# Two decoder layers on one core: the sampled rows' convolution, gate and pool moved into the mixing stage, the queries of sampled attention in an earlier memory pool, outputs issued by ScalarE and GpSimd

## The chip, the core and the metric

The kernel runs on one core of a Trainium2 chip, in one launch. The metric is the device time in microseconds (us). Before the change the median of three runs is 1473.05 us (1468.88 to 1478.08). TensorE, written PE in the profile, does the matrix products; VectorE (DVE), ScalarE (ACT) and GpSimd (POOL) work elementwise; SyncE (SP) only issues transfers (DMA). Every engine takes its instructions in the order in which they stand in its own list.

## What is computed

One step of a decoder with two layers, for 512 prompt rows and for 32 sampled rows (8 sequences of 4 new rows each), with 1024 columns. Of the reference:

```python
z = rms_norm(x, p['g_mix_pre']) @ p['w_in']
a, ga, u, vb, q, k, v, xd = jnp.split(z, IN_SPLITS, axis=-1)          # 256 columns each
ya, conv_new = conformer_conv(a, ga, conv_prev, ...)   # h = a*sigmoid(ga); depthwise conv of width 31; LayerNorm; silu
yb, v_rows = chunk_sgu(gelu(u), gelu(vb), ...)         # u * (causal mix of LayerNorm(v) within a chunk + b)
yc = (rms_norm(attend(q, k, v, lam), ...) * (1.0 - lam_init)).reshape(B_, T, D_C)   # differential attention
yd, pool_new = pool_mix(xd, pool_prev, pos, ...)       # means over windows of 2, 4, 8, 16 rows, minus the row
x = x + rms_norm(jnp.concatenate([ya, yb, yc, yd], axis=-1) @ p['w_out'], p['g_mix_post'])
gate, up = jnp.split(rms_norm(x, p['g_ffn_pre']) @ p['w_gu'], 2, axis=-1)
x = x + rms_norm((silu(gate) * up) @ p['w_down'], p['g_ffn_post'])
```

The sampled rows have states from earlier steps: the last 30 rows of the convolution's input, the last 15 of the pool's, and 2048 cached keys and values per sequence, in pages that a table names. The states after the step, the new keys and values and the normalized rows of the gate are outputs too.

## The kernel before

**Stages.** A layer has two stages. The mixing stage (`mixing`, pools `mix{l}`) makes the input projection and the four mixers of the 512 prompt rows. The projection carries the sampled rows along; their columns land in `zs` (128 partitions x 32 rows). The FFN stage (pools `ffn{l}`, `smp{l}`) has a main generator `prompt` (output projection, gate and up, down) and a background generator `sample`, whose steps are mixed into the steps of `prompt`. All matrix products are in fp32 made of parts: a weight `raw` is rounded to `whi` (ACT, L194) and the rest goes to `wlo` (DVE, or POOL for one piece, L197); an activation is split in the same way (L351 and L352 in the mixers, L241 and L242 in `turn`). A product is three matmuls: hi by hi, hi by lo, lo by hi.

**The output projection.** `project_last` runs it in eight turns, a row tile t and a half of the columns each, in the order (0,0), (1,0), (0,1), (1,1), (2,0), (2,1), (3,0), (3,1). The eight contraction blocks are taken in the order yc, ya, yd, yb, as the mixers get done. Each half's weights come in four pieces: of the second half POOL subtracts two, DVE two. After both halves of a row tile `finish` normalizes it, adds the residual (L1319), writes the rows x to memory (L1320), squares and scales again (L1326, tile m) and `turn` transposes it for the FFN (L239). Gate and up then run in chunks of 256 columns, with matmuls of 128x256.

**The sampled rows before.** `sample` first opens the pool `smx{l}` and runs `sample_conv`, `sample_gate` and `sample_pool` beside the output projection. The convolution adds 31 taps for two blocks of 128 channels by one small DVE instruction each (L894 twice, L897 60 times, 128x32); then two transposes, LayerNorm (L345, L346, L177 on DVE, L178 on POOL, L906), two transposes (L909) and the activation on ACT (L911). When `prompt` has set "turned" (the row tiles are transposed), the pool `att{l}` opens and `sample_attention` runs: queries (`rep`, `qs`), the new keys and values, then 64 gathers of key and value pages (L1011, L1041, POOL), transposing copies (L1014, `kt`), scores (`sx<-kt,qs`).

**What sets the order.** The instructions are written in the order in which the generators yield, and a scheduler with a model of the engines' times orders them on every engine. Pools share the core's memory: a tile that lies where an older one lay waits for the older one's last reader. Transfers issued by SP stand in one list: weight loads (`raw`, `rws`, `rwo`), row loads and, before the change, nearly all outputs.

## Time and profile before

| | value |
|---|---|
| three runs | 1468.88 to 1478.08 us, median 1473.05 |
| profiled execution | 1468.52 us |
| its span, first to last instruction | 1466.7 us |
| PE busy in it | 1399.7 us, 95% |
| DVE, ACT, POOL busy | 819.1, 498.2, 252.2 us |

The profile shows one execution. Busy times of engines overlap; a line of waits gives the idle time of an engine and the instruction that ended it. PEclk is the clock granted to TensorE as a share of its full speed. Times in a timeline are from the start of the span.

### The profile page before, as it was taken

What the parts mean: (1) busy time and instruction counts of PE and PEld (TensorE: products, weight loads), DVE (VectorE), ACT (ScalarE), POOL (GpSimd) and SP (SyncE); (2) the same over time, 40 slices, a digit from 0 to 9 for tenths busy, and PEclk for the clock granted to TensorE, in tenths of its full rate; (3) what the DMA queues carried; (4) which work ended last, traced back from release to release, by engine and by line L of the source; (5) the groups of instructions that cost most, each with busy time, mean ns of one, the idle gap of its engine ahead of it and who ended that gap; (6) DMA issues with size and microseconds to landing.
All of it is one profiled execution on the core that took longest, in us unless ns stands there. A gap on an engine that the chain in (4) does not pass through costs nothing.

```text
span 1466.7 us, 22999 instructions
## 1 busy us (share of the span) xinstructions
PE 1399.7 (95%) x9274; PEld 1091.6 (74%) x9274; DVE 819.1 (56%) x1624; ACT 498.2 (34%) x978; POOL 252.2 (17%) x271
## 2 busy tenths in 40 slices
PE   6999898999999999999989997989999999999997
PEld 6987687766676777777789876877666677777775
DVE  4996677866424323433769856778664333333344
ACT  4346453322224221222433444543222332222231
POOL 1001155354200000000310011543542000000003
PEclk9999898999999999999999978999999999999999
DMA  6320335787759741323432203367877596213132
GB/s 206 101 88 30 125 129 181 266 292 274 263 179 298 230 137 58 106 67 130 151 123 73 73 29 123 126 218 250 307 277 272 182 300 212 99 58 115 58 133 90
DMA packets 155204, 235.60 MB, mean 161 GB/s; under 512 B 8880, under 2 KB 116410, under 8 KB 155098
## 3 DMA queue, kind: packets, MB, share of 16 engines
q1 hardware_dynamic: 136522, 166.76, 34.6%
q0 software_dynamic: 18432, 67.12, 12.6%
q8 instruction: 73, 1.20, 0.3%
q14 instruction: 33, 0.27, 0.1%
q10 hardware_dynamic: 144, 0.26, 0.0%
HBM read 222.07 MB, written 12.04 MB: 160 GB/s over the span
## 4 chain that ended last, share of the span: by engine, by line
PE 80%; DVE 9%; issue 4%; DMA 2%; ACT 2%; POOL 2%; another core or an unknown queue 1%; SPq 0%; POOLq 0%; DVEq 0%; ACTq 0%
PE acc L128 61%; PE sx L128 10%; PE ps L128 3%; PE s L128 3%; DVE sca L897 2%; DVE wlo L197 1%; PE oT L128 1%; DMA kr<-in_cache_k_dram,ik 1%; POOL rsw L178 1%; DVE m L1326 1%; ACT whi L194 1%; DVE x_t L1319 1%; PE ps L521 1%; PE ps L239 1%
## 5 line engine op out<-in xcount | busy, mean ns | idle before, releaser
L128 PE MATMUL acc<-xhi,whi 128*128 128x512 f32 (+2 forms) x1152 | 410.8, 358 | 3.1 <-issue 1.1
L128 PE MATMUL acc<-xhi,wlo 128*128 128x512 f32 (+2 forms) x1152 | 407.9, 354 | 1.0 <-issue 0.7
L128 PE MATMUL acc<-xlo,whi 128*128 128x512 f32 (+2 forms) x1152 | 407.4, 354 | 1.3 <-DVE xlo L242 1.1
L197 DVE TENSOR_TENSOR wlo<-raw,whi 128x1024 fp32r<-128x1024 f32 x172 | 216.5, 1265 | 187.4 <-ACT whi L194 185.9
L194 ACT CAST whi<-raw 128x1024 fp32r<-128x1024 f32 x178 | 184.8, 1048 | 381.6 <-PE acc L128 324.0
L128 PEld LDWEIGHTS acc<-xhi,whi 128*128 128x128 f32 x1152 | 221.1, 192 | 47.5 <-issue 13.3
L128 PEld LDWEIGHTS acc<-xhi,wlo 128*128 128x128 f32 x1152 | 221.1, 192 | 34.9 <-issue 8.7
L128 PEld LDWEIGHTS acc<-xlo,whi 128*128 128x128 f32 x1152 | 221.3, 192 | 32.8 <-issue 5.3
L128 PE MATMUL acc<-whi,h 128*128 128x512 f32 x704 | 225.4, 397 | 0.3 <-issue 0.3
L128 PEld LDWEIGHTS acc<-whi,h 128*128 128x128 f32 x704 | 132.0, 189 | 45.4 <-issue 11.8
L128 PE MATMUL acc<-wlo,h 128*128 128x512 f32 x352 | 139.2, 397 | 0.0
L1301 POOL TENSOR_TENSOR m<-m,g_g_ffn_post 128x512 f32<-128x512 f32 x14 | 20.0, 1435 | 509.1 <-ACT junk L1300 509.1
L1014 DVE STREAM_TRANSPOSE kt<-kr 128x1024 f32<-128x1024 f32 x64 | 78.3, 1232 | 40.5 <-remote 18.2
L427 DVE SCALAR_TENSOR_TENSOR cacc<-hext,pf,cacc 128x512 f32<-128x512 f32 x120 | 86.9, 746 | 0.8
L1011 POOL DMA_INDIRECT kr<-in_cache_k_dram,ik x64 | 68.6, 1072 | 101.8 <-DVE kt L1014 88.1
L128 PEld LDWEIGHTS acc<-wlo,h 128*128 128x128 f32 x352 | 66.5, 189 | 17.6 <-issue 4.1
L178 POOL TENSOR_TENSOR rsw<-rsw,mhalf 128x1 f32<-128x1 f32 (+2 forms) x62 | 37.3, 604 | 239.4 <-DVE rsw L177 223.4
L1041 POOL DMA_INDIRECT vr<-in_cache_v_dram,iv x64 | 62.1, 970 | 82.0 <-PE sx L128 66.5
L1370 DVE SCALAR_TENSOR_TENSOR th<-th,acc 128x512 f32<-128x512 f32 (+1 forms) x46 | 29.7, 645 | 80.7 <-PE acc L128 80.5
L128 PE MATMUL sx<-kt,qs 128*32 128x128 f32 x1024 | 49.9, 277 | 7.7 <-issue 6.1
L128 PEld LDWEIGHTS sx<-kt,qs 128*32 128x32 f32 x1024 | 30.7, 109 | 24.5 <-issue 18.8
L1179 DVE SCALAR_TENSOR_TENSOR sth<-sth,ps 128x64 f32<-128x64 f32 x22 | 4.8, 219 | 72.7 <-ACT sth L1178 72.7
(426 smaller groups left out, 1855.2 us busy)
## 6 DMA issues: line engine op xcount, KB each, us to landing
raw<-in_w_gu_dram SPq DMA_DIRECT2D x44, 1024.0 KB
raw<-in_w_down_dram SPq DMA_DIRECT2D x20, 1024.0 KB
rws<-in_w_gu_dram SPq DMA_DIRECT2D x40, 512.0 KB
raw<-in_w_in_dram SPq DMA_DIRECT2D x16, 1024.0 KB
raw<-in_w_out_dram SPq DMA_DIRECT2D x8, 1024.0 KB
rwo<-in_w_out_dram SPq DMA_DIRECT2D x16, 512.0 KB
rws<-in_w_down_dram SPq DMA_DIRECT2D x16, 512.0 KB
x<-x_t SPq DMA_DIRECT2D x12, 512.0 KB
```

The source lines that it names most:

```text
L128: T.matmul(out, lhsT, rhs, start=start, stop=stop)
L178: G.tensor_tensor(y, v, mhalf[:P, :n], op=ALU.pow)
L194: S.copy(hi, src)
L197: eng.tensor_tensor(lo, src, hi.bitcast(F32), op=ALU.subtract)
L239: T.transpose(ov[:, c, :], src[:P, 128 * (4 * b + c):128 * (4 * b + c) + 128], ident[:P, :P])
L427: V.scalar_tensor_tensor(a, hext[c][:, t:t + SEQ], pf[:, 8 + 2 * t + c:9 + 2 * t + c], a, op0=ALU.mult, op1=ALU.add)
L897: V.scalar_tensor_tensor(a[:, c], ext[:, c, :, t:t + 4], pf[:, 8 + 2 * t + c:9 + 2 * t + c], a[:, c], op0=ALU.mult, op1=ALU.add)
L1011: G.indirect_dma_start(out=kr, out_offset=None, in_=ck, in_offset=bass.IndirectOffsetOnAxis(ap=ik[:, s, bg:bg + 1], axis=0))
L1014: V.transpose(kt, kr)
L1041: G.indirect_dma_start(out=v.rearrange("p t e -> p (t e)"), out_offset=None, in_=cv, in_offset=bass.IndirectOffsetOnAxis(ap=iv[:, s, a:a + ...
L1301: (V if (t, half) == (3, 1) else G).tensor_tensor(m[t][:, hs], m[t][:, hs], gain[:, hs], op=ALU.mult)
L1370: V.scalar_tensor_tensor(th[:, :n], th[:, :n], 0.5, ou[:, :n], op0=ALU.mult, op1=ALU.mult)
```

## The change

1. `sample_conv`, `sample_gate` and `sample_pool` no longer have a pool of their own. `mixing` runs them as its last step, after its own flows, in tiles of the mixing pool that are free by then (`spare`: the places of the queries' and keys' splits; `spare_p`: the ring `p`).
2. The convolution's 62 tap instructions become, for each block and each half of the sequences, one product over overlapping windows (128 x 16 outputs x 31 taps, L912) and one sum over the taps (L913), and two additions of the bias (L915).
3. The queries, the new keys and their scores become `sample_queries`, which runs in a pool `sqa{l}` before "turned"; `sample_attention` follows in `att{l}`, inside of it. `oacc` and `onew` take the places of `rep` and `se`.
4. Outputs of keys, values, states and of the rows x (for the three uses of `finish` that have a gain g) are issued by ACT, the sampled rows' loads and one output by POOL, no longer by SP.

The diff, cut to its core:

```diff
-
-    def sample_pool(l, mp, cmn, pw):
+        active += [sample_conv(l, mp), sample_gate(l, mp), sample_pool(l, mp, pw)]
+        while active:
+            advance(1)
+
+
+    def spare(mp, tag, n):
+        return mp.tile([128, SEQ], F32, tag=tag, name="sm_" + tag)[:, :n]
+
+    def spare_p(mp):
+        return mp.tile([128, SEQ], F32, tag="p", bufs=PB, name="smp")
+
+    def sample_pool(l, mp, pw):
         pf, _ = PF[l]
-        st = cmn.tile([128, 512], F32, tag="pr", bufs=2, name="sst")[:120, :256]
-        SY.dma_start(st, A["state_pool"][l].rearrange("s t c -> (s t) c"))
-        ext = mp.tile([128, 2, NS, 19], F32, tag="spx", name="spx")
+        st = spare_p(mp)[:120, :256]
+        G.dma_start(st, A["state_pool"][l].rearrange("s t c -> (s t) c"))
+        ext = spare(mp, "k1l", 38 * NS).rearrange("p (c s t) -> p c s t", c=2, s=NS)
         for c in range(2):
...
-        SY.dma_start(O[9][l].rearrange("s t c -> (s t) c"), cn[:120, :256])
+        S.dma_start(O[9][l].rearrange("s t c -> (s t) c"), cn[:120, :256])
...
-        SY.dma_start(O[10][l].rearrange("s t c -> (s t) c"), v_s)
+        G.dma_start(O[10][l].rearrange("s t c -> (s t) c"), v_s)
...
-    def sample_conv(l, mp, cmn):
+    def sample_conv(l, mp):
         pf, _ = PF[l]
-        ext = mp.tile([128, 2, NS, 34], F32, tag="scx", bufs=1, name="scx")
+        ext = [spare(mp, tag, 34 * NS).rearrange("p (s t) -> p s t", s=NS) for tag in ("k0l", "k1h")]
         for hf in range(2):
-            st = cmn.tile([128, 512], F32, tag="pr", bufs=2, name="sst")[:120, :256]
-            SY.dma_start(st, A["state_conv"][l, 4 * hf:4 * hf + 4].rearrange("s t c -> (s t) c"))
+            st = spare_p(mp)[:120, :256]
...
-            SY.dma_start(O[8][l, 4 * hf:4 * hf + 4].rearrange("s t c -> (s t) c"), cn[:120, :256])
+            S.dma_start(O[8][l, 4 * hf:4 * hf + 4].rearrange("s t c -> (s t) c"), cn[:120, :256])
             yield
-        a = mp.tile([128, 2, NS, 4], F32, tag="sca", name="sca")
-        for c in range(2):
-            V.tensor_scalar(a[:, c], ext[:, c, :, 0:4], pf[:, 8 + c:9 + c], pf[:, c:c + 1], op0=ALU.mult, op1=ALU.add)
-        for t in range(1, CW):
-            for c in range(2):
-                V.scalar_tensor_tensor(a[:, c], ext[:, c, :, t:t + 4], pf[:, 8 + 2 * t + c:9 + 2 * t + c], a[:, c],
-                                       op0=ALU.mult, op1=ALU.add)
-            if t % 4 == 0:
+        h = spare(mp, "k0h", 8 * NS + 256)
+        a = h[:, :8 * NS].rearrange("p (c s t) -> p c s t", c=2, s=NS)
+        for c in range(2):
+
+            k = pf[:, 8 + c:9 + c]
+            taps_ = bass.AP(k.tensor, k.offset, [k.ap[0], (0, 4), (0, 4), (2, CW)])
+            for hf in range(2):
+                e = ext[c][:, 4 * hf:4 * hf + 4]
+                win = bass.AP(e.tensor, e.offset, [e.ap[0], (34, 4), (1, 4), (1, CW)])
+                pr = spare_p(mp)[:, :16 * CW].rearrange("p (s t j) -> p s t j", s=4, t=4)
+                V.tensor_tensor(pr, win, taps_, op=ALU.mult)
+                V.tensor_reduce(a[:, c, 4 * hf:4 * hf + 4], pr, axis=AX, op=ALU.add)
                 yield
+            V.tensor_scalar(a[:, c], a[:, c], pf[:, c:c + 1], None, op0=ALU.add)
         o = ps()
         for c in range(2):
             T.transpose(o[:NT, 128 * c:128 * c + 128], a[:, c].rearrange("p s t -> p (s t)"), ident)
         mean, r = ln_stats(mp, o[:NT, :256], NT, "m")
-        xn = mp.tile([NT, 256], F32, tag="scn", name="scn")
+        xn = h[:NT, 8 * NS:]
...
-        with tc.tile_pool(name=f"smx{l}", bufs=1, reuse_waits="tile") as mp:
+        with tc.tile_pool(name=f"sqa{l}", bufs=1, reuse_waits="tile") as qp:
             yield
-            flows = [sample_conv(l, mp, sp), sample_gate(l, mp, sp), sample_pool(l, mp, sp, PW[l])]
-            while flows:
-                for fl in list(flows):
-                    if next(fl, 0) == 0:
-                        flows.remove(fl)
-                yield
+            pre = yield from sample_queries(l, sp, qp)
             while "turned" not in share:
                 yield
-        with tc.tile_pool(name=f"att{l}", bufs=1, reuse_waits="tile") as ap:
-            yield from sample_attention(l, sp, ap, ys, share)
+            with tc.tile_pool(name=f"att{l}", bufs=1, reuse_waits="tile") as ap:
+                yield from sample_attention(l, sp, qp, ap, ys, share, *pre)
...
-    def sample_attention(l, cmn, sp, ys, share):
+    def sample_queries(l, cmn, sp):
+
...
+        return sc, gsub, rep, nn, onew
+
+    def sample_attention(l, cmn, qp, sp, ys, share, sc, gsub, rep, nn, onew):
+        pf, nlam = PF[l]
+        ik, iv = IX[l]
+        selsq = sc[:, S_SQ:S_SQ + 256].rearrange("p (s t) -> p s t", s=NS)
+        qs = sp.tile([128, 4, 4, 2, 32], F32, name="qs")
+        G.memset(qs, 0.0)
+        nm = sp.tile([128, NS], F32, name="nm")
...
         V.scalar_tensor_tensor(x_t, m[t], r, x_t, op0=ALU.mult, op1=ALU.add)
-        SY.dma_start(x_at(stage + 1)(128 * t, 128), x_t)
         if g is None:
+            SY.dma_start(x_at(stage + 1)(128 * t, 128), x_t)
             return
         junk = jp.tile([128, DM], BF16, tag="ft", bufs=2, name="junk")
         S.activation(junk, x_t, AF.Square, accum_out=ss[:, 3:4])
+        S.dma_start(x_at(stage + 1)(128 * t, 128), x_t)
```

**What moves on ACT**, layer 0, at the end of the mixing stage. Before: the casts of the last mixer outputs (`ya`, `yb`), then the four casts of the second half of the output projection's weights, then the evacuation of its first turns (L1296, L1300).

```order
L351 CAST ya<-cacc_466 128x512
L351 CAST yb<-uv 128x512 x2
L351 CAST ya<-cacc_827 128x512
L194 CAST whi<-raw 128x1024 x4
L1296 COPY m_2039<-acc 128x512
L1300 ACTIVATE junk,sumt<-m_2039 128x512
L1296 COPY m_2040<-acc 128x512
```

After, from the same cast of `ya`: `smp`, `sm_...` are tiles of the sampled mixers, L835 is the last step of the pool, L926 an activation at the end of the convolution; L1312 is L1296 of before.

```order
L351 CAST ya<-cacc_827 128x512
L810 COPY smp<-ps 120x256
L811 DMA out_dram<-smp 120x256
L899 COPY smp<-ps 120x256
L900 DMA out_dram<-smp 120x256
L899 COPY smp<-ps 120x256
L835 ACTIVATE zs<-ps,pf_84 128x32 x2
L900 DMA out_dram<-smp 120x256
L926 ACTIVATE zs<-ps,pf_84 128x32 x2
L194 CAST whi<-raw 128x1024 x4
L1312 COPY m_2187<-acc 128x512
```

Three copies, three issues of outputs and four activations of the sampled rows now stand ahead of the four casts. The second of these casts also waits for the last sum of the taps (L913), whose product lies in the same memory, and the third for the landing of a state that L900 writes.

**What moves on PE**, layer 0, from the end of turn (1,0) of the output projection (blocks `yb`) to turn (0,1) (blocks `yc`). Before:

```order
L128 MATMUL acc<-whi,yb 128x512 x2
L128 MATMUL acc<-wlo,yb 128x512
L128 MATMUL acc<-whi,yb 128x512
L128 MATMUL acc<-whi,yc 128x512
L128 MATMUL acc<-wlo,yc 128x512
L128 MATMUL acc<-whi,yc 128x512 x2
L128 MATMUL acc<-wlo,yc 128x512
L128 MATMUL acc<-whi,yc 128x512
```

After: L897 transposes the convolution's state, L128 with `sm_q1h,pw` is the pool, L918 and L924 are the transposes before and behind the convolution's LayerNorm.

```order
L128 MATMUL acc<-whi,yb 128x512
L128 MATMUL acc<-wlo,yb 128x512
L897 MATMUL ps<-cst,smp 120x128
L128 MATMUL ps<-sm_q1h,pw 128x32
L128 MATMUL acc<-whi,yb 128x512 x2
L128 MATMUL acc<-wlo,yb 128x512
L128 MATMUL acc<-whi,yb 128x512
L918 MATMUL ps<-cst,sm_k0h 32x128 x2
L924 MATMUL ps<-cst,sm_k0h 128x32 x2
L128 MATMUL acc<-whi,yc 128x512
L128 MATMUL acc<-wlo,yc 128x512
```

The convolution's transposes have come ahead of the first matmul of turn (0,1).

**What moves on POOL**, layer 0, at the first gathers of sampled attention. Before: `scf` are copies of the convolution's state, L178 the reciprocal roots (128x1 for row tiles, 32x1 for the convolution's LayerNorm).

```order
L886 COPY scf<-scx 128x120
L178 TENSOR_TENSOR rsw<-rsw,mhalf 128x1
L886 COPY scf<-scx 128x120
L178 TENSOR_TENSOR rsw<-rsw,mhalf 128x1
L178 TENSOR_TENSOR rsw<-rsw,mhalf 32x1
L957 MEMSET qs 128x1024
L1011 DMA kr<-in_cache_k_dram,ik_2602 128x1024 x3
L1041 DMA vr<-in_cache_v_dram,iv_2603 128x1024 x4
```

After: L1317 is the gain of the output projection (L1301 before), the last L178 are those of the last row tile.

```order
L178 TENSOR_TENSOR rsw<-rsw,mhalf 128x1
L197 TENSOR_TENSOR wlo<-raw,whi 128x1024 x2
L178 TENSOR_TENSOR rsw<-rsw,mhalf 128x1
L1317 TENSOR_TENSOR m_2190<-m_2190,g_g_mix_post 128x512
L178 TENSOR_TENSOR rsw<-rsw,mhalf 128x1 x2
L1006 MEMSET qs 128x1024
L1027 DMA kr<-in_cache_k_dram,ik_2658 128x1024 x3
L1057 DMA vr<-in_cache_v_dram,iv_2659 128x1024 x4
```

The gathers stood behind the root of the convolution's LayerNorm; they stand behind the two roots of the last row tile now, and the first of them waits for the scaling of that row tile (L1343, which is L1326 before). Of the 256-column matmuls of gate and up, 188 stand ahead of the first scores before, 89 after; 48 stand ahead of the last row tile's turn after.

## Rows read from the trace of the kernel before

**Rows 1.** Page, part 1: busy time, share of the span, instructions of the matrix engine.

```profile
PE 1399.7 (95%) x9274; PEld 1091.6 (74%) x9274; DVE 819.1 (56%) x1624; ACT 498.2 (34%) x978; POOL 252.2 (17%) x271
```

**Rows 2.** Busy time by stretch: stretch, its length, five engines, PEclk, DMA share, GB/s.

```profile
core 0: us, PE busy (x) PEld busy (x) DVE busy (x) ACT busy (x) POOL busy (x), PEclk, DMA share, GB/s
176.00:183.00 7.00, 3.78 (x11) 2.76 (x11) 4.68 (x9) 5.76 (x10) 0.00 (x0) 0.52 0.99 343
183.00:189.00 6.00, 6.00 (x28) 4.93 (x27) 3.72 (x2) 4.51 (x7) 5.57 (x2) 1.00 0.04 10
230.00:241.00 11.00, 8.12 (x38) 7.86 (x39) 10.89 (x34) 5.19 (x15) 4.31 (x7) 0.53 0.72 230
```

**Rows 3.** Waits of PE, 160 to 275 us (layer 0): total us, times, longest.

```profile
PE ps L128 <- DVE ybs L862: 4.1, 1, 4.1
PE acc L128 <- ACT ya L351: 3.2, 1, 3.2
PE sx L239 <- DVE m L1326: 1.1, 2, 0.9
```

**Rows 4.** Waits of PE, 890 to 1005 us (layer 1).

```profile
PE sx L239 <- DVE m L1326: 2.4, 2, 1.8
PE ps L887 <- POOL scf L886: 1.3, 1, 1.3
```

**Rows 5.** Timeline of PE: start us, us, instruction, [idle before <-releaser].

```profile
179.79 0.80 PE L128 MATMUL acc<-whi,ya 128*128 128x512 f32 x1 [3.22 <-ACT ya L351]
...
189.47 0.40 PE L128 MATMUL acc<-whi,yc 128*128 128x512 f32 x1
...
227.19 0.28 PE L128 MATMUL acc<-xhi,whi 128*128 128x256 f32 x1
227.31 0.28 PE L128 MATMUL acc<-xlo,whi 128*128 128x256 f32 x1
...
244.17 1.09 PE L239 MATMUL sx<-cst,m 128*128 128x128 f32 x8
```

**Rows 6.** Timeline of ACT.

```profile
180.69 0.61 ACT L351 CAST ya<-cacc 128x512 fp32r<-128x512 f32 x1
182.30 3.89 ACT L194 CAST whi<-raw 128x1024 fp32r<-128x1024 f32 x4 [1.00 <-DVE ya L352]
...
250.18 0.65 ACT L911 ACTIVATE zs<-ps,pf 128x32 f32<-128x32 f32 x2 [1.58 <-PE ps L909]
```

**Rows 7.** Timeline of POOL.

```profile
183.43 5.77 POOL L197 TENSOR_TENSOR wlo<-raw,whi 128x1024 fp32r<-128x1024 f32 x2 [7.87 <-ACT whi L194]
...
245.48 0.53 POOL L178 TENSOR_TENSOR rsw<-rsw,mhalf 32x1 f32<-32x1 f32 x1 [2.68 <-DVE rsw L177]
...
247.10 1.20 POOL L1011 DMA_INDIRECT kr<-in_cache_k_dram,ik  x1 [0.19 <-issue]
...
349.27 0.94 POOL L1011 DMA_INDIRECT kr<-in_cache_k_dram,ik  x1 [0.30 <-issue]
```

**Rows 8.** Timeline of DVE.

```profile
235.96 2.03 DVE L897 SCALAR_TENSOR_TENSOR sca<-scx,pf,sca 128x32 f32<-128x32 f32 x12
...
242.83 1.28 DVE L1326 SCALAR_TENSOR_TENSOR m<-x_t,rsw,g_g_ffn_pre 128x1024 f32<-128x1024 f32 x1
...
244.37 0.41 DVE L345 BATCH_NORM_STATS2 bn<-ps 32x6 f32<-32x256 f32 x1
...
246.69 0.52 DVE L906 TENSOR_SCALAR scn<-ps,ag,rsw 32x256 f32<-32x256 f32 x1
...
355.36 1.25 DVE L1014 STREAM_TRANSPOSE kt<-kr 128x1024 f32<-128x1024 f32 x1 [0.22 <-DMA kr<-in_cache_k_dram,ik]
```

**Rows 9.** One line each: count, ns min/median/max, first and last start, form.

```profile
L352 DVE TENSOR_TENSOR ya<-cacc,ya x4: 681/686/692, 179.8 to 915.5; 128x512 fp32r<-128x512 f32 x4
...
L993 DVE TENSOR_REDUCE nn<-pn x2: 387/388/390, 271.1 to 1000.4; 32x8 f32<-32x256 f32 x2
...
L1317 ACTq DMA_DIRECT2D out_dram<-x_t x1: 370/370/370, 1463.2 to 1463.2; - x1
```

87 lines of the change are left out of this document (42 added, 45 removed).

## The prediction, made before the change was run

> **What bounds the kernel now.** I read the page's busy times first. TensorE (PE) is busy 95% of the span [rows 1], so an edit on another engine is worth what it takes from PE's idle time, or adds to it. All the sampled rows' matmuls, transposes and queries stay, in another place; PE's own work is the same. So I went to the waits of PE in the stretch that the change touches, from the end of the mixing stage to the first sampled attention scores. Layer 0 waits 3.2 us for ya, the last mixer output; 4.1 us for ybs, a sampled intermediate; 1.1 us for m, the rows that enter the FFN [rows 3]. Layer 1 waits 2.4 us for m and 1.3 us for scf of the sampled convolution [rows 4]; its wait for ya, at the same place, is taken to be as long. Last the windows, for the granted clock [rows 2]. After the stop before 179.79 the mean over 176 to 183 is 0.52, which is the lower level, 1.2 GHz, nearly throughout; over 183 to 189 it is 1.00 again, 2.4 GHz. After the 4.1 us stop it is 0.53 over 230 to 241. In that stretch PE is busy 8.12 us; the same work at 1.00 is 8.12 x 0.53 = 4.3, so **one drop costs about 3.8 us**. A reader should see that a stop of 3 to 4 us here is paid nearly twice.
>
> The sum is made against the profiled execution's 1468.5 us, which is 0.3% under the median of the runs, 1473.05.
>
> **The change part by part.**
>
> *1. The gaps at the head of the FFN go.* With the sampled mixers gone from there, the waits for ybs and scf have no place: -4.1 in layer 0 with its clock drop of 3.8, -1.3 in layer 1. Together **-9.2 us**.
>
> *2. The taps.* 62 small instructions become four products and four sums over 496 columns and two additions. Twelve of the old ones took 2.03 us [rows 8], 0.17 each, so 62 take 10.5. The nearest product is 0.69 for 512 columns; the nearest sum is 0.39 for 256 columns [rows 9], which is 0.39 if the columns cost nothing and 0.75 if they cost everything. I take 0.6 for each of the eight, one behind the other, and 0.3 for the additions: 5.1. No row has an operand that reads overlapping windows; at double price the products add 2.8 us. So VectorE (DVE) is relieved of some 5 us per layer; alone that moves nothing but what waits for it, which part 3 counts. The Trainium skill ("VectorE: DVE Perf Modes", Rules for kernel authors) asks for the fewest instructions in a chain of DVE work, which speaks for this, and warns that tensor_reduce runs at the 1x rate and is the slowest DVE operation, which speaks against it. Its table's 2293 ns for a product of 2048 columns gives 0.56 for 496, an estimate; by that the taps would take some 0.3 us less than 5.1.
>
> *3. The second half of the output projection's weights.* This is where the change costs. Before, ScalarE (ACT) rounds them at 182.30, four casts in 3.89 us, right behind the cast of ya [rows 6]; GpSimd (POOL) subtracts the first two low halves from 183.43, 5.77 us for two [rows 7]; PE arrives at turn (0,1) at 189.47 [rows 5] and doesn't wait. In the order of after, three copies and four activations of the sampled mixers and three DMA issues stand on ACT between the cast of ya and these casts, the last of them L926, behind the convolution's LayerNorm. PE too has the convolution's two pairs of transposes, L918 and L924, ahead of the first matmul of turn (0,1). An engine goes through its rows in order, so the cast can't start before the whole chain of taps, LayerNorm and activation is through. (Also the second cast's memory is that of the last product.) Its times, layer 0:
> - ya: four small copies, some 0.2 each, go ahead of its cast on ACT, and of the thirteen sampled transposes and small matmuls ahead of it on PE the last waits for a copy on POOL that waits for these. I take 1.4 for both: PE starts ya at 181.2 instead of 179.79. The thirteen themselves fill the gap.
> - PE: the two turns took 9.7 (179.79 to 189.47). With 11 small sampled matmuls between, 0.12 each by the pitch of the FFN's [rows 5], 1.3, they end at 192.2.
> - DVE: the products can start when ya's split and about ten small instructions are done, some of which wait for sampled matmuls that stand behind half of the ya matmuls: I put that at 187.5 (185.5 if nothing is waited for, 189 if every one is). Taps done at 192.6, just behind PE.
> - From there: transposes 0.4, statistics 0.41, small steps 0.3, reciprocal root on POOL 0.53 [rows 7], normalization 0.52, transposes 0.4, five hand-overs of 0.1: 3.1. L926 takes 0.65, as L911 does [rows 6], to 196.4. First cast 0.97 (3.89 / 4): 197.4. First low half on POOL 2.9 (5.77 / 2): 200.3. Second: 203.2.
> - PE does one matmul of the new turn at 197.4 and then stands till 200.3, so from 192.2 to 200.3, less 0.7 for L918, L924 and that matmul: **7.4 idle**. Five more at 0.23 (the pitch is 9.7 us over some 42), and it needs the second low half at 201.7: **1.5**.
> - The clock drops after such a stop: **3.8**, as measured after the 3.2 and the 4.1.
> Per layer **+12.7**; both layers have the same order here: **+25.4 us**. Bounds: zero, if the chain ends 8.1 us sooner; 2.8 more for slow windowed products.
>
> *4. The sampled queries and the early pool.* Queries, new keys and the values' part now run before "turned", beside the FFN's first chunks. PE work is the same. The gathers of the attention wait (the pool shares memory) for the scaling of m3 (L1343 now, L1326 before). At the gather of the steady phase 6.1 us lie from issue (349.27) to the copy that waited for its landing at 355.36 [rows 7, 8]; the transposing copy takes 1.25. From the scaling of m3: memset and issue 1.3, landing 6.1, copy 1.25: 8.6. PE in that time: eight transposes 1.1, then 41 gate and up matmuls at 0.12 (after has the first scores behind 89 of these matmuls and the turn of m3 behind 48), 4.9: 6.0. So 2.6, and 0.7 for the next two pages, **3.3 idle per layer, +6.6**. Before, the first gather went out at 247.10 and nothing waited. Bound below: zero, if PE arrives late for another reason.
>
> *5. m.* Turn m3 stood 17.0 us behind the end of the output projection (227.19 to 244.17) [rows 5]. In after it stands behind 48 of the 256-column matmuls (5.8 us), and squares, gain, two roots, residual (1.28 each for full rows [rows 8]) don't fit in that. I take layer 1's present 2.4 [rows 4] for both: **+1.3** in layer 0, none in layer 1.
>
> *6. Outputs and loads on other queues.* 14 output issues per layer move to ACT at 0.37 each [rows 9], 5.2 us, and about seven sampled loads to POOL at around 1 (an indirect one takes 0.94 to 1.20 [rows 7]). POOL is 17% busy, ACT 34% [rows 1]. Three of them are ahead of the casts, 1.1 us, but the casts wait for the convolution anyway: nothing; if that cover is gone, 1.1 per layer. SyncE gets its weight loads sooner; no wait of PE in these stretches is for a weight load [rows 3, 4], so nothing. The Trainium skill ("DMA: Bandwidth & Descriptors", Issuing engines are not separate DMA queues) says of spreading only that it saves the issuing sequencer's time. No run here shows it yet.
>
> Sum: -9.2 + 25.4 + 6.6 + 1.3 = **+24.1, 1468.5 to 1492.6**, 1493. On the median of the runs it would be 1497.
>
> **The rivals.**
> - *A, faster, 1450.* The splits find the convolution done: L926 ends by 188.3 (192.2 less a cast and a low half, 3.9) instead of 196.4. Then only part 1 stays, -9.2, with the gap before ya filled by the sampled matmuls that now stand there (1.4 per layer) and the gap behind m in layer 1 gone, 2.4, and its second drop avoided, 3.8: 1468.5 - 18. For it: DVE is only 4.7 of 7 us busy before 183 [rows 2], and the short chain may be started before ya. Against it: the order puts the taps behind ya's low halves. 0.12.
> - *B, about the same, 1478.* The chain ends 5 us sooner, 3.9 of the 8.9 idle us remain, and the gathers are nearly in time. Layer 0: -7.9 + 3.9 + 3.8 + 1.3 = 1.1; layer 1: -1.3 + 3.9 + 3.8 = 6.4; with one page's copy awaited in each, 1.25, 1478.5. For it: the starting time of the taps is the weakest number above. 0.33.
> - *C, forecast, 1493* (1482 to 1501): 0.43.
> - *D, worse, 1506.* Windowed products at double price (+2.8 per layer) and the wait for the gathers pulls the clock down once more per layer (+3.8): 1492.6 + 13.2. 0.12.
> - That the output moves pay for themselves needs a PE wait for a load; there is none, so it has no chance of its own.
>
> **How the numbers follow.** The time is C's. From A's 0.12 the low end leaves all out but its edge, 1463; the high end, 1506, leaves out the upper half of D: 0.18 outside. Within 1% (about what a measurement can tell; 1458 to 1488 round the median) lie B and a quarter of C: 0.44. Slower: the rest of C and D, 0.44. Faster: A, 0.12.
>
> **What would show it.** In the profile of after: no PE wait for ybs or scf (part 1); four products of 0.6 to 0.7 and four sums of at most 0.75 (2); PE's largest wait in the stretch at turn (0,1), for the low halves on POOL or the casts, 7 to 9 us, with the granted clock near 0.5 behind it (3); PE waiting 2 to 4 us for kt before the first scores (4) and 2.4 for m (5). I'm wrong if the casts L194 start by 190, or if the stop there is there and the clock stays at 1.00.

## The result and the profile after

The changed kernel takes 1509.2 us (median of four runs, 1507.2 to 1510.5) against 1472.3 us of the kernel before on the same chip: a ratio of 1.0256 [1.0230, 1.0281], slower. On a second chip, where the kernel before takes 1442.5, it is 1476.9, 1.0249 [1.0227, 1.0271]. The forecast was 1493 with a range up to 1506: right in the direction, too small by a third (+24 us where +37 came), and the measured time lies outside the range. Chips differ by 2% in the kernel before, so every ratio below is to it on the same chip.

Two pairs of profiles are compared, one for each chip: the *first pair* (before 1466.7 us, after 1508.8) and the *second pair* (both kernels unedited, 1441.8 and 1470.6). The PE line of the first pair's changed kernel answers to [rows 1]:

```profile
PE 1424.0 (94%) x9274; PEld 1101.2 (73%) x9274; DVE 805.1 (53%) x1520; ACT 498.0 (33%) x978; POOL 270.3 (18%) x285
```

The 9274 matmuls are the same in number, and PE is busy 24.3 us longer with them. From the page and the line of spans and clocks:

| us | before | after | difference |
|---|---|---|---|
| first pair: span | 1466.7 | 1508.8 | +42.1 |
| of it PE busy / not busy | 1399.7 / 67.0 | 1424.0 / 84.8 | +24.3 / +17.8 |
| mean granted clock; (1 - clock) x span | 0.979; 30.8 | 0.968; 48.3 | +17.5 |
| second pair: span | 1441.8 | 1470.6 | +28.8 |
| of it PE busy / not busy | 1385.7 / 56.1 | 1400.1 / 70.5 | +14.4 / +14.4 |
| mean granted clock; (1 - clock) x span | 0.982; 26.0 | 0.980; 29.4 | +3.4 |

(1 - clock) x span is what the lower clock can have cost at most, if PE had work all that time; as the clock has three digits, it is good to about 1 us. Without it the pairs agree: +24.6 and +25.4 us. But a single execution says little about the clock's share. On the second chip the four executions of the changed kernel lose 29.4 to 39.8 us in this way (median 36.9), and the profiled one least; seven of the kernel before lose 18.7 to 31.7 (median 23.1). So of the 34.5 us between the medians there, up to 13.8 can be the clock's, not 3.4.

The waits of PE in the first pair's changed kernel (waited for; us, times, longest), first layer 0, 160 to 275 us as in [rows 3], then layer 1, 890 to 1040 us, since it is later there than in [rows 4]:

```profile
PE sx L128 <- issue: 4.2, 6, 1.2
PE acc L128 <- ACT whi L194: 3.6, 1, 3.6
PE sx L239 <- DVE m L1343: 2.8, 2, 1.7
...
PE ps L924 <- DVE sm_k0h L921: 2.2, 1, 2.2
...
PE acc L128 <- DVE wlo L197: 0.9, 1, 0.9
...
PE sx L128 <- issue: 5.0, 6, 1.8
PE acc L128 <- ACT whi L194: 4.6, 2, 3.6
PE ps L461 <- DVE xn L455: 3.5, 2, 2.8
PE ps L924 <- DVE sm_k0h L921: 2.2, 1, 2.2
PE ps L918 <- DVE sm_k0h L915: 2.2, 1, 2.2
```

The waits for ya, ybs and scf are gone. In their place PE waits for the casts `whi` of the second half of the output projection's weights, and for the end of the sampled convolution (L915, L921), which it has to pass first. How that comes about stands in the timeline of the same kernel, layer 0 (start, duration, engine, line, what; in brackets the idle time ahead of it and who ended it):

```profile
188.84 1.26 DVE L912 TENSOR_TENSOR smp<-sm_k0l,pf 128x496 f32<-128x496 f32 x2
190.02 1.25 DVE L912 TENSOR_TENSOR smp<-sm_k1h,pf 128x496 f32<-128x496 f32 x2
191.19 2.39 DVE L913 TENSOR_REDUCE sm_k0h<-smp 128x16 f32<-128x496 f32 x4
195.77 0.53 DVE L921 TENSOR_SCALAR sm_k0h<-ps,ag,rsw 32x256 f32<-32x256 f32 x1 [0.68 <-POOL rsw L178]
196.44 0.39 PE L924 MATMUL ps<-cst,sm_k0h 32*128 32x32 f32 x2 [2.19 <-DVE sm_k0h L921]
196.87 0.65 ACT L926 ACTIVATE zs<-ps,pf 128x32 f32<-128x32 f32 x2 [3.25 <-PE ps L924]
197.41 3.88 ACT L194 CAST whi<-raw 128x1024 fp32r<-128x1024 f32 x4
198.58 5.67 POOL L197 TENSOR_TENSOR wlo<-raw,whi 128x1024 fp32r<-128x1024 f32 x2 [2.85 <-ACT whi L194]
200.37 1.64 DVE L197 TENSOR_TENSOR wlo<-raw,whi 128x1024 fp32r<-128x1024 f32 x1 [4.08 <-ACT whi L194]
200.39 0.80 PE L128 MATMUL acc<-whi,yc 128*128 128x512 f32 x1 [3.56 <-ACT whi L194]
```

Taps, LayerNorm, activation (L926), then the casts, 15.1 us later than in [rows 6]. PE starts turn (0,1) at 200.39; in [rows 5] it did so at 189.47.

What that costs is cut out best in the second pair: from the end of turn (1,0) to the end of turn (1,1), in both layers, before and after (stretch; length, PE busy, ..., PEclk, DMA share, GB/s):

```profile
189.40:201.30 11.90, 11.90 (x55) 9.52 (x54) 8.49 (x31) 4.73 (x12) 4.65 (x4) 1.00 0.39 128
908.00:920.05 12.05, 12.05 (x56) 9.72 (x55) 4.38 (x13) 4.01 (x11) 4.88 (x6) 1.00 0.65 206
```

```profile
190.00:215.03 25.03, 17.53 (x87) 13.52 (x86) 12.44 (x35) 10.70 (x24) 10.07 (x7) 0.86 0.56 198
922.00:948.04 26.04, 17.29 (x89) 13.33 (x88) 13.36 (x24) 9.33 (x22) 11.78 (x8) 0.80 0.58 191
```

Each layer loses 13 to 14 us here. PE stands 7.5 and 8.8 us, and its work takes 5.6 and 5.2 us longer. Of that 3.0 and 2.6 are matmuls of the sampled queries that have no place there in the kernel before; the groups of the same kernel in the first of the two stretches:

```profile
L128 PE MATMUL ps<-zs,se 128*128 128x32 f32 x16 | 1.9, 271 | 0.0
L128 PE MATMUL ps<-zs,qm 128*32 128x32 f32 x16 | 1.1, 199 | 0.9 <-ACT kn L971 0.9
```

The other 2.6 in each layer are what is left, and go with the clock, 0.86 and 0.80 here instead of 1.00. How late PE is (second pair, after less before, from the timelines):

| at | before | after | late by |
|---|---|---|---|
| last matmul of turn (1,0), layer 0 | 189.17 | 189.83 | 0.7 |
| first behind turn (1,1) | 201.30 | 215.03 | 13.7 |
| first gate and up matmul | 227.16 | 241.79 | 14.6 |
| first matmul of layer 1's projection | 726.05 | 738.81 | 12.8 |
| last matmul of turn (1,0), layer 1 | 907.99 | 922.19 | 14.2 |
| first behind turn (1,1) | 920.05 | 948.04 | 28.0 |
| end | 1441.8 | 1470.6 | 28.8 |

### The profile page after: what moved, and what is told of

It reads as the page before. It is cut to its first block, busy times and chain, and to the rows that moved or that the text cites. A ratio compares the mean times of both kernels' runs of the same rounds, so it can differ in the third digit from the quotient of the medians.

```text
span 1508.8 us, 22943 instructions
## 1 busy us (share of the span) xinstructions
PE 1424.0 (94%) x9274; PEld 1101.2 (73%) x9274; DVE 805.1 (53%) x1520; ACT 498.0 (33%) x978; POOL 270.3 (18%) x285
## 4 chain that ended last, share of the span: by engine, by line
PE 82%; issue 5%; DMA 5%; DVE 4%; ACT 2%; POOL 2%; SPq 0%; POOLq 0%; DVEq 0%; ACTq 0%
PE acc L128 62%; PE sx L128 10%; PE ps L128 3%; PE s L128 3%; DMA kr<-in_cache_k_dram,ik 1%; PE oT L128 1%; DVE wlo L197 1%; ACT whi L194 1%; PE ps L521 1%; POOL rsw L178 1%; DMA rws<-in_w_gu_dram 1%; DMA x_t<-in_x_prompt_dram 1%; DMA vr<-in_cache_v_dram,iv 1%; DVE x_t L1335 1%; PE ps L1042 0%
## 5 line engine op out<-in xcount | busy, mean ns | idle before, releaser
L128 PE MATMUL acc<-xhi,whi 128*128 128x512 f32 (+2 forms) x1152 | 412.8, 359 | 3.7 <-issue 1.5
L128 PE MATMUL acc<-xlo,whi 128*128 128x512 f32 (+2 forms) x1152 | 408.3, 355 | 3.0 <-DVE xlo L242 1.8
L128 PE MATMUL acc<-xhi,wlo 128*128 128x512 f32 (+2 forms) x1152 | 408.5, 355 | 0.5 <-issue 0.3
L128 PEld LDWEIGHTS acc<-xhi,whi 128*128 128x128 f32 x1152 | 220.9, 192 | 49.1 <-issue 16.8
L128 PEld LDWEIGHTS acc<-xlo,whi 128*128 128x128 f32 x1152 | 221.0, 192 | 37.7 <-issue 9.9
L128 PEld LDWEIGHTS acc<-xhi,wlo 128*128 128x128 f32 x1152 | 221.1, 192 | 36.2 <-issue 10.3
L128 PE MATMUL acc<-whi,h 128*128 128x512 f32 x704 | 222.9, 395 | 0.0
L128 PEld LDWEIGHTS acc<-whi,h 128*128 128x128 f32 x704 | 131.3, 188 | 41.3 <-issue 7.5
L128 PE MATMUL acc<-wlo,h 128*128 128x512 f32 x352 | 137.3, 393 | 0.0
L1317 POOL TENSOR_TENSOR m<-m,g_g_ffn_post 128x512 f32<-128x512 f32 x14 | 20.1, 1436 | 518.6 <-ACT junk L1316 518.6
L1030 DVE STREAM_TRANSPOSE kt<-kr 128x1024 f32<-128x1024 f32 x64 | 77.8, 1231 | 22.2 <-DMA kr<-in_cache_k_dram,ik 11.1
L178 POOL TENSOR_TENSOR rsw<-rsw,mhalf 128x1 f32<-128x1 f32 (+2 forms) x62 | 42.0, 680 | 250.4 <-DVE rsw L177 198.6
L128 PEld LDWEIGHTS acc<-wlo,h 128*128 128x128 f32 x352 | 66.1, 188 | 16.9 <-issue 3.3
L128 PE MATMUL sx<-kt,qs 128*32 128x128 f32 x1024 | 52.7, 286 | 18.7 <-issue 18.5
L128 PEld LDWEIGHTS sx<-kt,qs 128*32 128x32 f32 x1024 | 32.1, 112 | 35.2 <-issue 30.5
L128 PE MATMUL sx<-vr,pt 128*32 128x256 f32 x512 | 48.8, 384 | 0.2 <-DMA vr<-in_cache_v_dram,iv 0.2
```

The source lines that it names most:

```text
L128: T.matmul(out, lhsT, rhs, start=start, stop=stop)
L178: G.tensor_tensor(y, v, mhalf[:P, :n], op=ALU.pow)
L1030: V.transpose(kt, kr)
L1317: (V if (t, half) == (3, 1) else G).tensor_tensor(m[t][:, hs], m[t][:, hs], gain[:, hs], op=ALU.mult)
```

## The experiments

### Which part of the change costs

| kernel | what it has of the change | ratio to before |
|---|---|---|
| changed kernel, second chip | all | 1.0249 [1.0227, 1.0271] |
| e1_queries_late | all, but the queries behind "turned" | 1.0254 [1.0233, 1.0275] |
| e3_issue_sp | all, but the moved outputs and loads on SP | 1.0209 [1.0179, 1.0238] |
| e2_mixers_ffn | all, but the mixers in the FFN stage | 1.0128 [1.0107, 1.0149] |
| e4_taps_only | the short taps alone | 1.0073 [1.0047, 1.0099] |
| g2_taps_again | the same, another chip | 1.0058 [1.0038, 1.0077] |
| g1_pool_only | early pool and outputs alone | 1.0015 [0.9994, 1.0035] |

**e1_queries_late** undoes the early start of the queries, not their pool:

```diff
             yield
-            pre = yield from sample_queries(l, sp, qp)
             while "turned" not in share:
                 yield
+            pre = yield from sample_queries(l, sp, qp)
```

> The changed kernel, but the sampled queries and new keys run behind the turned rows again, as before the change; the mixers stay in the mixing stage. Theory M (the second half of the output projection's weights waits for the sampled convolution, 11 to 12 us per layer with its clock drop; the rest of the loss is the head of the FFN, where scores are waited for): the stop of 6 to 9 us at turn (0,1) stays; the queries' own work falls out of the output projection into the head of the FFN. If scores that come early are what costs there, 1495 to 1502 us; the rival, that the gathers' wait for the last row tile costs it whatever the queries do, gives 1505 to 1512.

The ratio stays what it was, so the time of the queries has no measurable part in the loss. The expectations of these first four runs are in the times of the first chip: 1.0254 is 1510 us there, in the range of the rival.

**e2_mixers_ffn** puts the three mixers back into the FFN stage, with their short taps, in a pool `smx{l}` ahead of `sqa{l}`:

```diff
-        active += [sample_conv(l, mp), sample_gate(l, mp), sample_pool(l, mp, pw)]
-        while active:
-            advance(1)
...
+        with tc.tile_pool(name=f"smx{l}", bufs=1, reuse_waits="tile") as mp:
+            yield
+            flows = [sample_conv(l, mp), sample_gate(l, mp), sample_pool(l, mp, PW[l])]
```

> The changed kernel, but the three sampled mixers run in the FFN stage beside the output projection, as before the change, with the new short taps, the early queries and the outputs on ScalarE and GpSimd. Theory M: the stop at turn (0,1) is gone in both layers, some 24 us less than the changed kernel, less what the mixers cost at the head of the FFN: 1475 to 1488. Rival Q (early queries and the early pool are the loss) and rival I (issuing on ScalarE and GpSimd is the loss): 1500 or more.

On the first chip's scale this is 1491 us, far from the rivals' 1500 or more and just above the 1475 to 1488 of theory M. On the chip of this run the whole change was not timed; e1 stands for it. By that the move of the mixers is worth 1.0254 - 1.0128 = 1.26%, 17 us: half of the loss, and close to the forecast's parts 3 and 1 together, 25.4 - 9.2 = 16.2.

**e3_issue_sp** turns each moved issue back:

```diff
-            S.dma_start(O[8][l, 4 * hf:4 * hf + 4].rearrange("s t c -> (s t) c"), cn[:120, :256])
+            SY.dma_start(O[8][l, 4 * hf:4 * hf + 4].rearrange("s t c -> (s t) c"), cn[:120, :256])
...
```

> The changed kernel with every output and sampled load issued by SyncE again. Theory M: same as the changed kernel, 1505 to 1512, since the casts wait for the convolution whatever else stands ahead of them. Rival I: 1495 or less.

Some 0.4% less than e1, the full change but for the queries, on the same chip; the intervals overlap by a hair. On the first chip's scale it is 1503 us, between the two expectations. The issues are at most a small part.

**e4_taps_only** and **g2_taps_again** are the kernel before with the eight products and sums in place of the 62 instructions:

```diff
-        for t in range(1, CW):
-            for c in range(2):
-                V.scalar_tensor_tensor(a[:, c], ext[:, c, :, t:t + 4], pf[:, 8 + 2 * t + c:9 + 2 * t + c], a[:, c],
-                                       op0=ALU.mult, op1=ALU.add)
...
+                V.tensor_tensor(pr, win, taps_, op=ALU.mult)
+                V.tensor_reduce(a[:, c, 4 * hf:4 * hf + 4], pr, axis=AX, op=ALU.add)
+            V.tensor_scalar(a[:, c], a[:, c], pf[:, c:c + 1], None, op0=ALU.add)
```

> The kernel before with one edit: the 62 tap instructions become four products, four sums and two additions, at their old place. Theory M: VectorE is relieved of some 5 us per layer where it was full at the head of the FFN, so the waits for ybs and m (4.1 and 1.1 us in layer 0, 2.4 and 1.3 in layer 1) and one clock drop of 3.8 shrink: 1462 to 1469. Rival: the taps hide beside the output projection, 1470 to 1475.

> The kernel before with the short taps alone, as in the run that gave 1.0073 [1.0047, 1.0099], now on the chip of the run beside it. Theory T: 1.0073 again, within 1.004 to 1.010. Rival (the loss was that chip's): within 0.002 of 1.

Slower on both chips, by under 1% but clear of 1 in both intervals, against the expectation that a shorter chain on DVE helps or does nothing: on the first chip's scale e4 is 1483 us, beyond both of its ranges. The edit does help at the head of the FFN (the wait for ybs is gone, and the clock's mean is 0.982 to 0.989, median 0.987, against 0.984 in the kernel before on the same chip), and the loss is elsewhere. The groups of PE's sampled matmuls show where (busy, mean ns of one). First the kernel before of the second pair, then the short taps alone:

```profile
L128 PE MATMUL sx<-vr,pt 128*32 128x256 f32 x512 | 44.9, 383 | 1.3 <-DMA vr<-in_cache_v_dram,iv 1.3
L128 PE MATMUL sx<-rws,hs_in 128*32 128x256 f32 x320 | 23.4, 384 | 0.0
```

```profile
L128 PE MATMUL sx<-vr,pt 128*32 128x256 f32 x512 | 58.6, 384 | 0.0
L128 PE MATMUL sx<-rws,hs_in 128*32 128x256 f32 x320 | 27.0, 385 | 0.0
```

These matmuls have weights of 32 columns. Where they stand together in PE's list, they start four at a time, within 0.02 us, and the next four 0.22 us later (second pair's kernel before, from 333.38), so four run beside one another. One takes as long in both kernels, but the 512 value products (`vr`) cover 13.7 us more; they come in 88 groups between other products, where there were 59 (counted in the timelines). No line of theirs was edited. Two things in the edit can have moved them, and no run parts the two: DVE is free earlier, and the convolution's generator yields 4 times instead of 7, which by itself can shift how the sampled steps are mixed in.

**g1_pool_only** is the early pool and the outputs with the old taps in the FFN stage.

> The kernel before with the queries in the early pool and the outputs on ScalarE and GpSimd, but with the mixers in the FFN stage and the 62 old tap instructions: the kernel of the run with the mixers put back (1.0128), less the short taps. Theory T (the parts add up: short taps 0.73%, early pool and outputs the rest, mixers in the mixing stage 1.2%): 1.0128 less 0.0073 = 1.0055, between 1.003 and 1.009. Rival P (the early pool and outputs cost all of the 1.28%, and the short taps nothing beside them): 1.0105 to 1.0145. Rival O (what counts is the order in which the page products are mixed in, which each edit shuffles; the value products stand in 37 groups in this kernel's list of TensorE against 59 in that of before): at most 1.001.

The loss is too small to be told from none; P is out, and T's bounds are missed. The parts do not add up: pool and outputs 0.15%, taps 0.6 to 0.7%, both together 1.28% (e2). O fits best, but less than its text says: its 37 groups were counted in the list and its 59 in a timeline; timeline by timeline it is 54 against 59, so nearly the order of before, and nearly its time:

```profile
L128 PE MATMUL sx<-vr,pt 128*32 128x256 f32 x512 | 43.3, 382 | 0.9 <-DMA vr<-in_cache_v_dram,iv 0.8
```

In e2 the same products cover 54.2 us in 76 groups, in the changed kernel 49.5 in 63 (second pair). In e1 they cover 57.1 in 73, with the same ratio as the changed kernel, so their time alone does not decide the total.

### The stop at turn (0,1)

**e8_splits_first** lets the casts of the second half go ahead of the sampled activations:

```diff
+                with tc.high_priority(URG if half == 1 and turns is W_OUT_TURNS else 0):
+                    prs[half] += raw_rows(w, k0 + g, min(4, K - g), 512 * half, G if k0 + g == 0 and half == 1 else V, rings[half][g // 4],
+                                          also and also(half))
```

> The changed kernel with a higher priority for the second half of the output projection's weight casts: on ScalarE the four casts L194 now stand ahead of L926, else nothing moves there. Theory M: the casts start 4 us sooner, at the end of the taps, the stop of TensorE at turn (0,1) falls from 6.6 to about 3 us per layer: 7 to 10 us less than the changed kernel, a ratio of 1.019 to 1.021. Rival: the casts are held by memory or by the landing of the states that ScalarE writes, and the time stays.

1.0258 [1.0233, 1.0282]: nothing is gained. The taps begin at 188.81, as in the first pair's changed kernel, and the casts 4.9 us behind them instead of 8.6 (8.6 in the second pair's changed kernel too, where the taps begin at 184.84). But the stop goes to the low halves on DVE, and is 6.1 us in all instead of 6.6:

```profile
193.66 3.88 ACT L194 CAST whi<-raw 128x1024 fp32r<-128x1024 f32 x4
195.68 4.65 POOL L197 TENSOR_TENSOR wlo<-raw,whi 128x1024 fp32r<-128x1024 f32 x2
196.63 7.00 DVE L197 TENSOR_TENSOR wlo<-raw,whi 128x1024 fp32r<-128x1024 f32 x2 [0.37 <-ACT whi L194]
...
200.49 4.29 POOL L1318 TENSOR_TENSOR m<-m,g_g_mix_post 128x512 f32<-128x512 f32 x2 [0.16 <-DMA g_g_mix_post<-in_g_mix_post_dram]
201.47 0.79 PE L128 MATMUL acc<-wlo,yc 128*128 128x512 f32 x1 [3.94 <-DVE wlo L197]
```

Two subtractions, whose median over the kernel before is 1.2 us each, take 7.0 while POOL works on tiles of its own. Nor can PE start the turn before L924, which stands ahead of it in PE's own list and still waits 2.2 us for the convolution.

**e5_filler** keeps PE at work through the stop, with 2 x 8 matmuls that nothing reads, one set behind L918 and one behind L924:

```diff
+        f = ps()
+        for i in range(8):
+            mm(f[:NT, :128], a[:, 0].rearrange("p s t -> p (s t)"), ident)
...
+        for i in range(8):
+            mm(f[:128, :256], xn[:, 0:128], xn)
```

> The changed kernel with matmuls added that nobody reads: eight of 32x128 behind L918 and eight of 128x256 behind L924, from the convolution's own tiles, so that they run in the two stops of TensorE ahead of turn (0,1). Theory M with the clock: the stops are filled, the clock stays at 1.00 behind them where it fell to 0.5 for 10.2 and 13.7 us, and the time falls by 2 to 3.5 us per layer, to a ratio 0.003 to 0.005 under that of the changed kernel, although work was added. Rival: the clock falls for another reason, or costs nothing there; then the time stays, or rises by up to 2 us.

1.0277 [1.0250, 1.0304]: no gain, against theory M; whether it is slower than the changed kernel (1.0249 on the same chip), the intervals leave open. PE is busy 22.8 of the 25 us there instead of 17.5, and the clock is no better; from 206 to 210 it is 0.50, right behind 5.9 us of filler that PE did without a gap:

```profile
190.00:215.00 25.00, 22.80 (x96) 17.77 (x94) 15.95 (x33) 9.45 (x21) 10.35 (x7) 0.80 0.44 140
...
206.00:210.00 4.00, 4.00 (x10) 3.14 (x10) 4.00 (x2) 3.07 (x9) 4.00 (x2) 0.50 0.53 198
```

A wait of 2.2 us remains ahead of the transposes of L924, and the filler of 5.9 us is longer than the stop of 3.6 that it was to fill. So the clock's part of the 13 us could not be measured apart; it stays at the 2.6 us per layer read from the windows.

### The order of the page products

If the loss outside of the output projection is one of order, what decides is how fast the sampled steps are mixed into gate and up. `PACE_A` sets that: the share of each main step's cost that counts towards the next background step while gate and up run (0.8 in both kernels).

```diff
-PACE_A = 0.8
+PACE_A = 0.7
```

> As e4_taps_only, but the background steps are mixed in at 0.6 in place of 0.8 of the main steps' cost: 171 changes of tile in place of 234. Theory S: 0.996 to 1.001. Rival: 1.005 to 1.010.

> The changed kernel, with the background steps mixed in at 0.7 in place of 0.8: in TensorE's order 148 changes between full tiles and the narrow ones of the cached pages in place of 202; the mixers and the casts stay as they are. Theory S (narrow matmuls that stand alone between full ones cost more than in rows of 16, about 0.17 per change): 9 us less than the changed kernel, ratio 1.016 to 1.020; the loss in the output projection, some 15 us per layer, stays. Rival: the order of the pages costs nothing, 1.023 to 1.027.

> The kernel before, with the one edit of e14_after_pace: background steps at 0.7 in place of 0.8. The rows of cached values' matmuls in TensorE's order: 33 in place of 38 (in e14_after_pace 18 in place of 46). Theory S (rows that are broken up cost; so far 68 rows gave 1.0073, 56 gave 1.0002, 40 gave 0.990 with the short taps): some 0.6 us per row, 5 rows, 0.996 to 1.000. Rival P: the pace itself helps every kernel by as much as it helped the changed one (from 1.025 to 0.991): 0.963 to 0.972.

> The kernel before with background steps at 0.5: 24 rows in place of 38, 172 changes of tile in place of 164. Theory S by rows: 0.988 to 0.995. Rival: by changes of tile alone, 1.000 or more.

> The short taps alone (e4_taps_only) with background steps at 0.5: 26 rows in place of 68. Theory S by rows: below the 0.990 of e13_pace (40 rows), 0.980 to 0.988. Rival: the gain stops at some row length, 0.988 to 0.993.

> The changed kernel with the sampled mixers back beside the output projection (e2_mixers_ffn, 1.0128) and background steps at 0.5: 26 rows in place of 53. Theory M and S together: without the stop at turn (0,1) it must be faster than e14_after_pace (0.991) by most of the 1.2% that the mixers cost there: 0.976 to 0.986. Rival: the stop's cost is not additive, 0.988 to 0.995.

| parts of the change | 0.8 | 0.7 | 0.6 | 0.5 |
|---|---|---|---|---|
| none | 1 | 0.9895 [0.9871, 0.9920] | | 1.0038 [1.0012, 1.0064] |
| short taps | 1.0073, 1.0058 | | 0.9903 [0.9867, 0.9939] | 0.9896 [0.9855, 0.9937] |
| all but the mixers' move | 1.0128 | | | 0.9952 [0.9924, 0.9981] |
| all | 1.0249 to 1.0256 | 0.9912 [0.9878, 0.9947] | | |

Theory S, by rows or by changes of tile, held in none of these. The changed kernel at 0.7 (0.9912) and the short taps at 0.6 (0.9903) are faster than it or its rival allowed, and the kernel before at 0.7 (0.9895) lies between its two ranges. For the kernel before and the short taps at 0.5 (1.0038, 0.9896) the rivals held; without the mixers' move (0.9952) the rival is missed by a hair. So neither count is shown to be the rule.

The short taps cost 0.6 to 0.7% at 0.8 and gain 1.4% at 0.5. At 0.7 the whole change costs 0.2%, inside the intervals, though its stop at the output projection is there as before. PE's waits from 185 to 215 us of that kernel:

```profile
PE acc L128 <- ACT whi L194: 3.6, 1, 3.6
PE ps L924 <- DVE sm_k0h L921: 2.2, 1, 2.2
PE acc L128 <- DVE wlo L197: 0.9, 1, 0.9
```

Compared with the kernel before at 0.7 (on another chip) it is 15.8 us late behind the output projection of layer 0, and only some 4 at the end: most is given back while the page products run. They cover less there than in any other run:

```profile
L128 PE MATMUL sx<-vr,pt 128*32 128x256 f32 x512 | 32.8, 380 | 0.3 <-DMA vr<-in_cache_v_dram,iv 0.3
```

The grouping is not the whole rule. The kernel before at 0.5 has these products in 24 groups (35.7 us) and is still slower than at 0.7, and its sampled rows are late at the other end. Of PE's waits over the whole span, these two do not occur at 0.7:

```profile
PE ps L271 <- DVE m_s L263: 14.2, 2, 7.1
...
PE sx L128 <- DMA raw<-in_w_gu_dram: 8.2, 2, 4.1
```

The first of these is the sampled rows' own last step, twice, with nothing beside it.

**e10_values_first** tried to get the grouping by priority, in the kernel with the short taps:

```diff
+                with tc.high_priority(URG):
+                    for t in range(4):
+                        for a, v in enumerate(vs_, a0):
+                            mm(ops[32 * a:32 * a + 32, :256], pt[:, t, a], v[:, t, :], start=(t == 0), stop=(t == 3))
```

> The kernel before with the short taps (as in e4_taps_only, 1.0073), and a higher priority for the matmuls of the cached values, so that the 16 of a sequence stand closer together: 177 changes between full and narrow tiles in TensorE's order in place of 234 (164 in the kernel before). Theory S: 57 changes fewer, at 0.2 each 11 us: ratio 0.997 to 1.001. Rival: the short taps cost for another reason, 1.005 to 1.010.

1.0002 [0.9981, 1.0024]: in the range of theory S, on a chip where the taps alone were not timed. But in the trace the value products stand in 85 groups instead of 88 and cover 54.2 us instead of 58.6, so the grouping hardly came, and that it took the loss away is not shown.

**e9_switches** asks whether the change between wide and narrow weights costs by itself. The kernel before gets an unread product of 32 columns ahead of each of 72 products of 256 or 288 columns; the trace shows each as two matmuls:

```diff
+            if k == 0 and n <= 288:
+                mm(o[:32, 480:512], ident[:, :32], ident[:, :32], start=True, stop=True)
```

> The kernel before, with one matmul that nobody reads ahead of each of the 72 products of 256 or 288 columns (input projection, first chunk of gate and up): 128x32 weights, 32 columns, so a small tile between full ones. Theory S: every change between a full 128x128 tile and a 32-wide one costs TensorE some 0.2 us (in the traces a 256-column matmul ahead of a small one takes 0.33 instead of 0.12, a small one ahead of a full one 0.31 instead of 0.06): 72 x 0.45 = 32 us more, ratio 1.018 to 1.025. Rival: a matmul of 32 columns costs its columns, some 0.03, and the time rises by 2 to 4 us, ratio under 1.004.

1.0103 [1.0069, 1.0137], some 15 us, between the two expectations, so neither range holds. The starts in the trace show what a pair costs where it stands between full matmuls:

```profile
43.77 0.29 PE L128 MATMUL acc<-xhi,wlo 128*128 128x288 f32 x1
43.99 0.25 PE L128 MATMUL acc<-cst 128*32 128x32 f32 x2
44.17 0.39 PE L128 MATMUL acc<-xhi,whi 128*128 128x256 f32 x1
44.39 0.28 PE L128 MATMUL acc<-xlo,whi 128*128 128x256 f32 x1
```

From the first to the last of these lines it is 0.62 us; without the pair it would be 0.25, a step of 0.13 behind a matmul of 288 columns and of 0.12 behind one of 256. So a pair costs 0.37 us (median of the 33 that stand so), which makes 12 of the 15 us. The others fall into a wait or stand beside other narrow or small matmuls. Theory S had the kind of cost right; its sum took 0.45 for all 72.

Real narrow matmuls pay at the same edges: a full matmul of 512 columns takes 0.326 us to the start of a narrow one behind it, and the first full one behind narrow ones 0.337 to the next, against 0.23 between full ones (medians, second pair's kernel before). The Trainium skill ("TensorEngine Tiling (Array Packing)", Key Properties) says that a change of the tiling mode drains TensorE; these starts agree.

## Why the prediction was wrong

**Part 3, the main term, held.** It said +12.7 us per layer: 8.9 idle and 3.8 for the clock. The second pair shows 7.5 and 8.8 idle (0.9 of the 7.5 a wait of the queries) and 2.6 that go with the clock, 10.1 and 11.4, somewhat less than forecast. The casts were to start at 196.4, and PE to begin turn (0,1) in earnest at 200.3; in the first pair these stand at 197.41 and 200.39. Which step gates was said wrongly: PE waits for the third cast, whose rows the first block (yc) uses, and then 0.9 us for DVE's low half, not for POOL's. That the last time came out nearly equal is luck: the third cast ends when POOL's first low half was to end. What the forecast did not have in this stretch are the queries' matmuls, 3.0 and 2.6 us; it had put them beside the FFN's first chunks.

**Part 2's duration held, its effect did not.** Four products start at 188.84 and end at 191.27 (0.61 each) and four sums take 2.39 (0.60 each), 4.7 us together against 4.8 taken for these eight. The trace does not bear out a sum that is slower than the product. "Alone that moves nothing but what waits for it" is **the first step that failed**: the new taps alone, with no other edit, cost 0.6 to 0.7%, some 9 us, and what they moved is the order in which the page products come into PE's list.

**Part 1 held in the place and failed in the sum.** No wait for ybs or scf is left, and the clock over 230 to 241 is 1.00 in the first pair's changed kernel instead of 0.53 in [rows 2]:

```profile
230.00:241.00 11.00, 9.88 (x49) 7.88 (x48) 7.21 (x11) 9.81 (x19) 7.91 (x6) 1.00 0.42 158
```

But from the first gate and up matmul to the start of layer 1, PE's lag falls by 14.6 - 12.8 = 1.8 us only, where parts 1, 4 and 5 in layer 0 made it -7.9 + 3.3 + 1.3 = -3.3.

**Part 4: the waits came, not the cost.** The copies of the first pages are waited for, 5.9 us in the second pair's changed kernel (kt, L1030) against 6.6 forecast. In the first pair the profile names no releaser for them ("issue" above), and there the second drop of the clock follows that rival D priced. The timeline and the windows of that kernel:

```profile
254.15 1.07 PE L239 MATMUL sx<-cst,m 128*128 128x128 f32 x8 [1.72 <-DVE m L1343]
254.89 1.31 POOL L1027 DMA_INDIRECT kr<-in_cache_k_dram,ik  x1 [1.30 <-ACT h L1389]
...
259.57 1.25 DVE L1030 STREAM_TRANSPOSE kt<-kr 128x1024 f32<-128x1024 f32 x1
260.97 0.64 PE L128 MATMUL sx<-kt,qs 128*32 128x128 f32 x16
261.84 2.54 DVE L1030 STREAM_TRANSPOSE kt<-kr 128x1024 f32<-128x1024 f32 x2 [1.03 <-DMA kr<-in_cache_k_dram,ik]
```

```profile
252.00:264.00 12.00, 8.47 (x76) 6.90 (x75) 10.03 (x41) 1.56 (x4) 8.43 (x10) 1.00 0.61 204
264.00:276.00 12.00, 8.97 (x55) 6.72 (x55) 1.62 (x3) 1.48 (x3) 3.68 (x3) 0.57 0.66 260
```

In the second pair this drop did not come (clock 1.00 from 252 to 276). Yet g1, which has the early pool without the rest, costs 0.15%, not the 7.9 us of parts 4 and 5. Its profile has waits, 1.4 us for kt and 10.6 for m, where the second pair's kernel before has 3.7 for m; but PE is busy 9.5 us less (1376.2 against 1385.7).

**Part 6** forecast nothing for the moved outputs; e3 leaves at most 0.4%, and its interval overlaps that of e1.

**The step that failed in the sum** is a sentence of the first paragraph: "PE's own work is the same". The idle time was forecast at -5.4 + 17.8 + 6.6 + 1.3 = +20.3 us, and PE's time not busy rose by 17.8 and 14.4 (the waits for ya went too, 6.4 us in the second pair, which the forecast had not counted as a gain). PE's busy time was forecast to rise by 3.8, the clock's balance; it rose by 24.3 and 14.4 for the same matmuls. Two things are in that. One is the overlap of narrow matmuls: in the second pair the value products cover 4.6 us more (49.5 against 44.9) and those of `rws` 1.7 (25.1 against 23.4). The other is the clock, at most 3.4 us net in the second pair, 13.8 between the medians of that chip, and 17.5 in the first pair: one fixed price for a drop, paid at two foreseen places, does not hold it, since the changed kernel's own loss differed by 10.4 us among four executions on one chip. In the second pair the two leave some 5 of the 14.4 us unplaced, even if all of its clock loss counts.

**What stays open.** By what rule the order of the page products turns into time: the number of groups goes with the time that the value products cover, but not with the total. A price per edge is shown (e9), and with the short taps PE's weights change between widths or heights of 32, 64 and 128 in 519 places, in the kernel before in 445 (counted in the traces). But with the short taps at 0.6 it is 453, and that kernel is 1% faster than the one before. And at 0.7 the changed kernel recovers its late start in that phase by a way that was not followed. Nor is the clock's share in the stop shown apart.

**Rivals.** A and B needed the convolution done 8 and 5 us sooner, and it was not. D's second clock drop came in the first pair, and nearly D's time (1506 against 1509). That is no proof of D: its slow windowed products did not come, and in the second pair, with the same ratio, the second drop did not either.

The fastest are the kernel before at a pace of 0.7 (0.9895 [0.9871, 0.9920]) and the short taps at 0.5 (0.9896 [0.9855, 0.9937]), which cannot be told apart; the short taps at 0.6 (0.9903) and the changed kernel at 0.7 (0.9912), on other chips, lie within the same intervals.

## What to carry to other kernels

Placing a step ahead of others in an engine's list costs what stands behind it there: here four weight casts stood behind a serial chain of small sampled steps, 10 to 11 us in each layer, which the trace of before gave to within a quarter. But with a scheduler that mixes two streams, "the same work in another place" is a claim about order that the list must show: count in it how often narrow matmuls are parted from their group, for the part of the kernel that the edit doesn't touch as well. An edit worth 1% has a sign only at a given pace; before it is judged, the pace is to be tried again with it.
